# Nearest-neighbour upsampling: a first load split by partitions, and other sizes for three stores

## The chip, the cores and the metric

The kernel runs on one core of a Trainium2 chip. The time is device microseconds of that core; a shorter time is better. An execution taken by the hardware profiler has a span, from its first to its last instruction, which is a little shorter than the time.

## The reference

Every element of a float32 image batch `x[16, 64, 64, 64]` is written four times, to a 2 x 2 block of the output `[16, 64, 128, 128]`:

```
for i in range(new_h):
    for j in range(new_w):
        src_i = i // scale_factor
        src_j = j // scale_factor
        result[:, :, i, j] = x[:, :, src_i, src_j].copy()
```

There is no arithmetic. 16.78 MB are read and 67.11 MB are written.

## The kernel before

The 65,536 image rows of 64 floats are cut into 128 runs of 512 rows, one for each partition of the on-chip memory. A row is 256 B as input and becomes 1024 B of output (two output rows of 128 floats). So a load of n rows moves n x 256 B into each partition it names, and a store of k rows moves k x 1024 B out of each partition.

All of it lies in one on-chip buffer, `whole` (lines 188 to 190). Its upper part, `xt`, takes the whole input, 512 rows for each partition. The output tiles are built below it and, as input rows are used up, on top of them: even tiles at the bottom, odd tiles ending where the unread input begins (line 208). The assertion in line 209 holds two neighbouring tiles apart, and with it bounds the size of a tile and the next one together.

The loads (lines 194 to 197) are three DMAs on SyncE's queue (SP): 32 rows of all partitions, then 256, then 224. `begin_before_barrier` (line 13) puts the first three DMAs of SP (`EARLY`, line 10) ahead of the barrier with which all engines start, so that they begin at once.

The loop in line 206 runs over the nine entries of `rows` (line 181). For tile n, VectorE copies k input rows, each element twice and each row twice (`expanded`, line 199), into the tile: in one instruction (line 217), or in two where `k0` is set (lines 214 to 217). Then a DMA stores the tile (line 219). Tiles 0, 1 and the last are stored from SP's queue, the other six from ScalarE's (ACT). A DMA is issued by the sequencer of SP or ACT after it has waited for the copy. Transfers of one queue follow each other on each DMA engine, and the two queues share the 16 DMA engines.

What orders the work: a copy waits for the load that brings its rows, and for the store two tiles back, whose place it takes. In the kernel before, the 1-row copy waits for the first load, the 53-row copy for the second, and the sixth tile's for the third; the third tile's copy waits until the first store has landed. `close_early` (line 80) arranges the end of the program around the last store, and isn't touched.

Of the kernel before, what the change touches and what calls it, by code (L numbers as in the profile page):

```python
# [153 lines left out]
@with_exitstack  # L154
def kernel(
    ctx: ExitStack,
    tc: tile.TileContext,
    x: bass.AP,
    scale_factor: int,
    out: bass.AP,  # L160
):
    nc = tc.nc
    nc.at_finalize(begin_before_barrier)
    nc.at_finalize(close_early)
    P = nc.NUM_PARTITIONS
    s = int(scale_factor)
    B, C, H, W = x.shape
    R = B * C * H // P
    fdt = x.dtype

    xp = x.rearrange("b c h w -> (b c h) w").rearrange("(p r) w -> p r w", p=P)
    op = out.rearrange("b c (h hd) w -> (b c h) (hd w)", hd=s).rearrange(
        "(p r) w -> p r w", p=P
    )

    rows = [54, 38, 54, 60, 54, 62, 64, 62, 64]
    GROW = s * s
    FREE = 79
    WF = FREE * GROW * W
    assert sum(rows) == R
    mem_pool = ctx.enter_context(tc.tile_pool(name="mem", bufs=1))
    LEAD = 32
    whole = mem_pool.tile([P, LEAD + WF + R * W], fdt, name="mem")
    mem = whole[:, LEAD:]
    xt = mem[:, WF:].rearrange("p (r w) -> p r w", r=R)  # L190

    HEAD = 32
    cuts = [0, HEAD, R // 2 + HEAD, R]
    for lo, hi in zip(cuts, cuts[1:]):
        nc.sync.dma_start(out=xt[:, lo:hi], in_=xp[:, lo:hi])  # L197

    def expanded(r0, r1):
        return (  # L200
            xt[:, r0:r1].unsqueeze(2).unsqueeze(4).to_broadcast([P, r1 - r0, s, W, s])
        )

    r0 = 0
    before = (0, 0)
    for n, k in enumerate(rows):
        size = k * GROW * W
        at = 0 if n % 2 == 0 else WF + r0 * W - size
        assert at >= before[1] or at + size <= before[0]
        before = (at, at + size)  # L210
        u = mem[:, at : at + size].rearrange(
            "p (k a w b) -> p k a w b", k=k, a=s, w=W
        )
        k0 = 1 if n == 0 else 0
        if k0:
            nc.vector.tensor_copy(out=u[:, :k0], in_=expanded(r0, r0 + k0))  # L216
        nc.vector.tensor_copy(out=u[:, k0:], in_=expanded(r0 + k0, r0 + k))  # L217
        issuer = nc.sync if n in (0, 1, len(rows) - 1) else nc.scalar
        issuer.dma_start(out=op[:, r0 : r0 + k, :], in_=u)
        r0 += k  # L220
# [35 lines left out]
```

## Time and profile before

| | |
|---|---|
| median of 3 runs | 197.16 us (197.07 to 197.19) |
| span of the profiled execution | 195.8 us |
| VectorE busy | 76.9 us, 10 copies |
| DMA | 83.89 MB in 12 transfers, mean 429 GB/s |

The three runs give the time of whole executions; the profiled execution is known by its span, 1.36 us below their median. In the views, DVE is VectorE, SPq and ACTq are the sequencers of SyncE and ScalarE, POOL is GpSimd. A row with DMA names a transfer by destination and source: `mem<-in_x_dram` is a load, `out_dram<-mem` a store. The queue q1 is SP's and q10 ACT's. A share of the DMA is the mean over the 16 DMA engines. The rows with xcount group instructions of one line and shape: busy time in all, mean ns of one, then the idle time of the engine before them and what ended it. The rows of issues give KB of a transfer and the time from issue to landing.

### The profile page before, as it was taken

How to read it: one execution, taken by the hardware profiler on the slowest of the kernel's cores; microseconds unless marked ns; L12 is line 12 of the kernel's file. 1: busy time of each engine (PE TensorE's matmuls, PEld its weight loads, DVE VectorE, ACT ScalarE, POOL GpSimd, SP SyncE). 2: the span in 40 equal slices, each digit the busy share in tenths (PEclk: the TensorE clock that was granted, in tenths of full speed). 3: DMA queues.
4: the chain of work that ended last, by engine and by line, in shares of the span. 5: the costliest groups of instructions: out<-in, count | busy, mean ns of one | idle time of the engine just before them, and what ended most of it. 6: DMA issues, size and time to landing. Idle time of an engine off the chain costs nothing.

```text
span 195.8 us, 76 instructions
## 1 busy us (share of the span) xinstructions
DVE 76.9 (39%) x10; POOL 0.2 (0%) x4
## 2 busy tenths in 40 slices
DVE  0000099990029287059008805920790079000000
POOL 0000000000000000000000000000000000000000
DMA  9999989989898988999999899999999999999994
GB/s 429 429 429 429 402 375 539 398 362 542 362 435 382 551 373 362 542 402 402 402 537 407 362 542 415 415 415 415 429 429 429 429 415 558 473 435 422 429 429 214
DMA packets 1728, 83.89 MB, mean 429 GB/s; under 512 B 192, under 2 KB 192, under 8 KB 192
## 3 DMA queue, kind: packets, MB, share of 16 engines
q10 hardware_dynamic: 864, 46.66, 55.0%
q1 hardware_dynamic: 864, 37.22, 44.2%
HBM read 16.78 MB, written 67.11 MB: 429 GB/s over the span
## 4 chain that ended last, share of the span: by engine, by line
DMA 61%; DVE 24%; SPq 0%; issue 0%
DMA out_dram<-mem 49%; DVE mem L217 24%; DMA mem<-in_x_dram 12%; SPq L197 0%
## 5 line engine op out<-in xcount | busy, mean ns | idle before, releaser
L217 DVE COPY mem<-mem 128x13824 f32<-128x13824 f32 (+5 forms) x9 | 76.6, 8515 | 84.6 <-DMA out_dram<-mem 65.6
L216 DVE COPY mem<-mem 128x256 f32<-128x256 f32 x1 | 0.3, 293 | 4.8 <-DMA mem<-in_x_dram 4.8
L237 POOL MEMSET const-bfloat16-1.0<- 128x1 bf16 x1 | 0.1, 102 | 0.0
L237 POOL MEMSET const-uint8-127<- 128x1 uint8 x1 | 0.1, 101 | 0.0
L237 POOL MEMSET const-float32-0.0<- 128x1 f32 x1 | 0.1, 98 | 0.2 <-issue 0.2
L237 POOL MEMSET const-float32-1.0<- 128x1 f32 x1 | 0.1, 98 | 0.0
## 6 DMA issues: line engine op xcount, KB each, us to landing
out_dram<-mem ACTq DMA_DIRECT2D x2, 7936.0 KB, 31.6
out_dram<-mem ACTq DMA_DIRECT2D x2, 6912.0 KB, 23.7
out_dram<-mem ACTq DMA_DIRECT2D x1, 7680.0 KB, 26.1
mem<-in_x_dram SPq DMA_DIRECT2D x1, 7168.0 KB, 40.2
out_dram<-mem SPq DMA_DIRECT2D x1, 6912.0 KB, 19.0
out_dram<-mem SPq DMA_DIRECT2D x1, 4864.0 KB, 25.2
mem<-in_x_dram SPq DMA_DIRECT2D x1, 1024.0 KB, 4.8
mem<-in_x_dram SPq DMA_DIRECT2D x1, 23.7
```

What stands on the lines that cost most here:

```text
L216: nc.vector.tensor_copy(out=u[:, :k0], in_=expanded(r0, r0 + k0))
L217: nc.vector.tensor_copy(out=u[:, k0:], in_=expanded(r0 + k0, r0 + k))
L237: nc = _bacc.Bacc("TRN2", target_bir_lowering=False, num_devices=1)
```

## The change

The first 256 rows now come in two DMAs that part the partitions and not the rows: all 256 rows of partitions 0 to 15, then all 256 rows of partitions 16 to 127. The third brings the other 256 rows of all partitions. The first tile has 63 rows (54 before), the second 31 (38) and the last 62 (64). The first tile is copied in one instruction; a tile with an odd number of rows other than the first, which is the second alone, is copied as one row and the rest.

```
-    rows = [54, 38, 54, 60, 54, 62, 64, 62, 64]
+    rows = [63, 31, 54, 60, 54, 62, 64, 62, 62]
...
-    HEAD = 32
-    cuts = [0, HEAD, R // 2 + HEAD, R]
-    for lo, hi in zip(cuts, cuts[1:]):
-        nc.sync.dma_start(out=xt[:, lo:hi], in_=xp[:, lo:hi])
+    LANES = 16
+    HALF = R // 2
+    for p0, p1, lo, hi in (
+        (0, LANES, 0, HALF),
+        (LANES, P, 0, HALF),
+        (0, P, HALF, R),
+    ):
+        nc.sync.dma_start(out=xt[p0:p1, lo:hi], in_=xp[p0:p1, lo:hi])
...
-        k0 = 1 if n == 0 else 0
+        k0 = 0 if n == 0 else k % 2
         if k0:
             nc.vector.tensor_copy(out=u[:, :k0], in_=expanded(r0, r0 + k0))
         nc.vector.tensor_copy(out=u[:, k0:], in_=expanded(r0 + k0, r0 + k))
```

## The prediction

> **What bounds the kernel now.** I read the page first: engine shares, the slices of the span, the DMA queues and the chain.
>
> ```profile
> span 195.8 us, 76 instructions
> ...
> DVE 76.9 (39%) x10; POOL 0.2 (0%) x4
> ...
> DMA  9999989989898988999999899999999999999994
> GB/s 429 429 429 429 402 375 539 398 362 542 362 435 382 551 373 362 542 402 402 402 537 407 362 542 415 415 415 415 429 429 429 429 415 558 473 435 422 429 429 214
> DMA packets 1728, 83.89 MB, mean 429 GB/s; under 512 B 192, under 2 KB 192, under 8 KB 192
> ...
> q10 hardware_dynamic: 864, 46.66, 55.0%
> q1 hardware_dynamic: 864, 37.22, 44.2%
> HBM read 16.78 MB, written 67.11 MB: 429 GB/s over the span
> ```
>
> VectorE (DVE) works 39% of the span. The 16 DMA engines work 55.0 + 44.2 = 99.2% of it, in every slice but the last. Jumps in the GB/s row (375, then 539) are whole packets counted in one slice. The packet row tells how transfers are shared out: 192 small packets are 12 transfers (3 loads, 9 stores) times 16 engines, so each transfer ends on all 16; the other 1728 - 192 = 1536 are 12 x 128, one for each partition of a transfer. One engine thus carries 8 partitions of each 128-partition transfer. A view by stretches gives the steady rate (columns: stretch, length, DVE, POOL, clock, DMA share, GB/s):
>
> ```profile
> 5.00:24.00 19.00, 0.12 (x1) 0.00 (x0) 1.00 1.00 435
> 24.00:39.00 15.00, 14.86 (x2) 0.00 (x0) 1.00 0.99 428
> 166.00:190.00 24.00, 0.41 (x1) 0.00 (x0) 1.00 1.00 431
> ```
>
> Loads alone run at 435 GB/s with a share of 1.00, that is 27.2 GB/s for each engine, and stores alone at 431. All bytes at 435 GB/s need 83.89 / 0.435 = 192.9 us of the 195.8 us span: 2.9 us are left for start, slower first packets and end, and no rearrangement can win more. Losses have no such bound: any time in which the engines move less than 27.2 GB/s each is added to the end, because each later transfer gives every engine the same 8 partitions again.
>
> Next the chain in order of time, the copies by shape, and the issues:
>
> ```profile
> 0.43 23.65 DMA mem<-in_x_dram
> 24.09 0.02 issue
> 24.11 14.30 DVE mem L217
> 38.41 0.02 issue
> 38.42 19.01 DMA out_dram<-mem
> 57.44 0.02 issue
> 57.46 7.37 DVE mem L217
> 64.83 0.02 issue
> 64.85 20.38 DMA out_dram<-mem
> ```
>
> ```profile
> L217 DVE COPY mem<-mem 128x16384 f32<-128x16384 f32 x2 | 17.4, 8694 | 18.6 <-DMA out_dram<-mem 18.6
> L217 DVE COPY mem<-mem 128x15872 f32<-128x15872 f32 x2 | 16.9, 8427 | 21.0 <-DMA out_dram<-mem 21.0
> L217 DVE COPY mem<-mem 128x13824 f32<-128x13824 f32 x2 | 14.7, 7360 | 21.9 <-DMA out_dram<-mem 21.9
> L217 DVE COPY mem<-mem 128x13568 f32<-128x13568 f32 x1 | 14.3, 14286 | 19.0 <-DMA mem<-in_x_dram 19.0
> L217 DVE COPY mem<-mem 128x9728 f32<-128x9728 f32 x1 | 5.2, 5226 | 0.0
> L216 DVE COPY mem<-mem 128x256 f32<-128x256 f32 x1 | 0.3, 293 | 4.8 <-DMA mem<-in_x_dram 4.8
> ```
>
> ```profile
> mem<-in_x_dram SPq DMA_DIRECT2D x1, 7168.0 KB, 40.2
> out_dram<-mem SPq DMA_DIRECT2D x1, 4864.0 KB, 25.2
> mem<-in_x_dram SPq DMA_DIRECT2D x1, 1024.0 KB, 4.8
> mem<-in_x_dram SPq DMA_DIRECT2D x1, 23.7
> ```
>
> ```profile
> 0.00 1.33 SPq L197 DMA_DIRECT2D mem<-in_x_dram  x3
> ...
> 38.42 5.60 SPq L219 DMA_DIRECT2D out_dram<-mem  x2
> ```
>
> The chain names a 14.30 us copy, but the DMA engines are busy under it: the third load, issued near 0.9 us (three issues in 1.33 us), lands 40.2 us later, at 41.1, and the first store is issued at 38.42. That copy is covered with 41.1 - 38.4 = 2.7 us to spare. It is slow because its 53 rows are odd: 14286 / 13568 = 1.053 ns an element, where the 54-row form has 7360 / 13824 = 0.532.
>
> **The change, part by part.** *Instructions.* SP still issues three loads and three stores, ACT six stores, in the same order; VectorE still has ten copies. Transfers stay 12, issue cost is unchanged, and the packets become 16 + 112 + 128 + 9 x 128 + 192 = 1600 if the 16- and the 112-partition load still use all 16 engines. Edits to copies and stores cost nothing as long as loads run at the old rate:
>
> First copy, now 63 odd rows in one instruction: 16128 x 1.053 = 16.98 us (if it took the rate of the even form, 8.6). It waits for both first loads, 8.39 MB instead of 9.44: at the old rate they land 1.05 / 0.435 = 2.4 us before 24.09, at 21.7. So the first store goes out at 38.7 instead of 38.42, covered by the third load, whose end stays at 41.1. Without that cover each microsecond of lateness costs one.
>
> The 1-row copy (0.29 us) leaves the first tile and goes to the second: 0.29 + 7680 x 0.532 = 4.4 us instead of 5.23. Its store queues behind the first store on SP and is covered by it. The third copy waits for the first store to land and runs 7.37 us under the second store. That store lands now at 43.7 + 25.2 = 68.9 (its issue is the last 0.3 us of the two-issue row), 4.0 us after the issue at 64.85; with 31 rows for 38 it is 7 x 1024 x 128 / 0.435 = 2.1 us shorter, leaving 1.9 us for the start of a transfer. The first load, with 2.41 us of bytes, landed after 4.8, so start and landing together take 2.4 us; at worst 0.5 us shows, and I take 0. The wait for the third load moves from the sixth to the fifth tile, at 85 us, long after either landing. The last store loses 2 rows (0.6 us), but the sum of rows is the same: 0.
>
> *First load, 16 partitions.* Each engine gets one 65,536 B row, in place of eight short ones. No row of this trace shows a transfer that writes few partitions, so I bound it. If 27.2 GB/s is a limit of the engine, the load takes 65,536 / 27.2 = 2.41 us as now: 0. If it is a limit of the way into each group of 8 partitions, sixteen partitions lie in anything from 2 to 16 groups, and 16 engines share as many ways: 19.3, 9.6, 4.8 or 2.4 us. A rate in proportion to partitions, 435 / 8 = 54 GB/s, gives 19.3 too. I take four ways, the middle rung of the crowded ones (2, 4, 8): 9.6 us, +7.2, with 0 and +16.9 as ends. Every engine is in it, and the second load waits behind it on the same queue, so all of it is added.
>
> [...]
>
> *Second load, 112 partitions.* Seven rows to an engine, 7 x 2.41 = 16.9 us if nothing is shared. If the engines stay four to a way, 7 x 9.6 = 67.5. In a 128-partition load eight rows belong to each engine, and the trace shows no sharing; with seven, blocks of partitions no longer match the groups of eight, and two engines meet on one way part of the time. I take half of the time for the slowest engine: 16.9 x 1.5 = 25.3, +8.4, with 0 and +50.6 as ends. Nearest to the 435 GB/s row is 0, but the same premise that slows the first load forbids it: 16 partitions are missing, so other ways carry more than their share.
>
> [...]
>
> *Third load.* 128 partitions, eight to an engine: 19.3 us as at 435 GB/s. It covers the 17.0 us copy even then, with 2.3 us for issue and start. At the start, eight short rows become one long one: the page's first slices already show 429 GB/s, against 435 later, which over 20 us leaves 0.3 us to win; I take -0.2 (0 to -0.5).
>
> **Sum.** 195.8 + 7.2 + 8.4 - 0.2 = 211.2 us of span. The median of the runs is 197.16, 1.36 above the span; with that kept, 212.6 us.
>
> **Rivals.**
> - *No crowding* (the other side): 27.2 GB/s belongs to the engine and not to the partitions written. For it: 435 and 431 GB/s in both directions look like one engine limit. Against it: a limit on the receiving side would give the same row. Then all edits are covered, and the time is 197.2 with -0.5 to +0.5: 197.0. It decides if the first load lands within 6 us.
> - *Only the first load crowds.* If engines spread the 112 partitions well, the groups with all eight partitions left still need 8 x 2.41 = 19.3 us: +7.2 and 0 to +2.4, so 204.4 to 206.8; 205.5.
> - *Both stay four to a way.* 7.2 + 50.6: 255 us. For it: consecutive partitions on the 16 engines at any one time; against it: that needs rows dealt out one by one, which nothing in the trace shows.
> - *The slow copy comes out of cover*: if the third load's end does not move with the second load's landing, the 17.0 us copy starts late and the DMA idles. With the second load landing at 37, the copy ends at 54 and the slowest engine has load until 37 + 19.3 = 56: 2 us short of deciding. It would add 1 to 3 us to the forecast, within its range.
>
> **How the numbers follow.** Both loads crowded, as summed, with its sharing uncertain by 5 us below and 8 above (207 to 220): 0.52. Only the first: 0.20. Heavier than 220: 0.08. No crowding: 0.20, of it 0.10 faster by over 0.2%, 0.08 within 0.2% and 0.02 slower; 0.2% or 0.4 us is what a measurement of this kernel can tell from no change. So faster 0.10, same 0.08, slower 0.82. The likeliest case's own range is 207 to 220; to leave out no more than 2 in 10 the range must reach the uncrowded case too: 196.7 to 220.
>
> **What would show it.** Right: the first load lands near 12 us instead of 4.8, the second near 37 instead of 24, the first eight GB/s slices well below 429, the packet row at 1600 with 192 small ones, the first copy at 17.0 us, and later stretches unchanged at 431 to 435 GB/s but with gaps on engines that were ahead. Wrong: 435 GB/s in the first 20 us with the second load landed by 22. Fewer than 192 small packets would mean that a load doesn't use all 16 engines, and then its share would have to be told anew.

## The result, and the profile after

| | before | changed |
|---|---|---|
| median of 5 runs | 197.16 us (197.04 to 197.26) | 219.34 us (219.10 to 219.78) |
| span of the profiled execution | 195.8 us | 217.8 us (its time 219.10) |

The ratio is 1.1129, with a 95% interval of 1.1115 to 1.1142: the change costs 22.2 us. The forecast was 212.6 us, in a range of 196.7 to 220.0: the time lies inside it by 0.7 us, and 6.7 us above the forecast.

The page of the changed kernel, the rows that answer to those shown of before:

```profile
span 217.8 us, 78 instructions
...
DMA  9985999898988988999989997999898989989984
GB/s 193 193 193 193 349 205 217 337 409 385 409 379 379 557 376 385 491 396 437 501 384 440 424 488 345 488 396 536 373 409 385 554 380 396 536 373 396 536 373 210
DMA packets 1601, 83.89 MB, mean 385 GB/s; under 512 B 193, under 2 KB 193, under 8 KB 193
...
q10 hardware_dynamic: 864, 46.66, 49.5%
q1 hardware_dynamic: 736, 37.22, 49.0%
q14 instruction: 1, 0.00, 0.0%
```

The DMA engines are as busy as before, 98.5% of the span. But for eight slices, 44 us, they move 193 to 349 GB/s. A busy DMA engine isn't a fast one: a 64 KB packet of the first load took 7.9 to 9.2 us, where one of the second load took 2.42 before. The packets are 1600 as counted out, and one of another queue (q14).

The chain of waits of the changed kernel (start, length, what):

```profile
0.45 42.84 DMA mem<-in_x_dram
43.28 0.03 issue
43.31 0.02 DVEq L221
43.33 0.05 issue
43.38 16.95 DVE mem L221
60.34 0.03 DVE mem L220
60.36 21.11 DMA out_dram<-mem
81.47 0.02 issue
81.49 7.37 DVE mem L221
88.86 0.02 issue
88.89 19.06 DMA out_dram<-mem
```

and its first and third load among the issues (the last column is the time from issue to landing), with the stretch in which the second load runs (length, DVE, POOL, clock, DMA share, GB/s):

```profile
mem<-in_x_dram SPq DMA_DIRECT2D x1, 11.8
...
mem<-in_x_dram SPq DMA_DIRECT2D x1, 61.6
```

```profile
10.40:39.70 29.30, 0.00 (x0) 0.00 (x0) 1.00 0.86 215
```

(A stretch counts a packet where it starts, and the second load's first row started before 10.40 on every engine. Its 7.34 MB in about 31 us are 237 GB/s.)

The first megabyte lands after 11.8 us where it took 4.8: +7.0. The second load lands at 43.28. The third, issued near 0.9, lands at 62.5, after the first store's issue at 60.36: by the landings, the 16.95 us copy is covered still. The third load landed at 41.1 before, so 21.4 of the 22.0 us of span are lost by then.

### The profile page after: what moved, and what is told of

Read it like the earlier page. It is cut to its first block, busy times and chain, and to the rows that moved or that the text cites. A ratio compares the mean times of both kernels' runs of the same rounds, so it can differ in the third digit from the quotient of the medians.

```text
span 217.8 us, 78 instructions
## 1 busy us (share of the span) xinstructions
DVE 78.1 (36%) x10; POOL 0.2 (0%) x4
## 4 chain that ended last, share of the span: by engine, by line
DMA 64%; DVE 22%; SPq 0%; issue 0%; DVEq 0%
DMA out_dram<-mem 44%; DVE mem L221 22%; DMA mem<-in_x_dram 20%; SPq L201 0%; DVEq L221 0%; DVE mem L220 0%
## 5 line engine op out<-in xcount | busy, mean ns | idle before, releaser
L221 DVE COPY mem<-mem 128x15872 f32<-128x15872 f32 (+5 forms) x9 | 78.0, 8663 | 110.7 <-DMA out_dram<-mem 67.3
```

## The experiments

### The loads alone, and the rest alone

Two runs part the diff. One puts the loads together again and keeps all else of the change:

```
-        (0, LANES, 0, HALF),
-        (LANES, P, 0, HALF),
+        (0, P, 0, 32),
+        (0, P, 32, HALF),
         (0, P, HALF, R),
```

> The split by partitions is taken back (32 rows, 224 rows, 256 rows, each of all 128 partitions); row counts, copies and stores stay as changed. If the split alone costs the time: 197.2 us, 196.6 to 197.7, second load landing 21 to 22 us, first copy 17.0 us and covered. If the odd 63-row copy, the 31-row second store or the 62-row last store carry a part: 199 us or more.

Measured: 198.10 us beside 197.13, ratio 1.0046 (1.0029 to 1.0063), between its two cases. The other puts the three new loads into the kernel before and nothing else (its `rows` and `k0` stay):

> The kernel before with the three loads of the change and nothing else of it. If the split by partitions is the whole loss but for the 0.9 us seen with the loads merged: 218.2 to 219.2 us, second load landing at 43 us. If the changed row counts take part in the loss beyond that 0.9 us: 217 us or less.

Measured: 218.91 us, ratio 1.1103 (1.1084 to 1.1121). Its second load lands as late as in the changed kernel, or a little later (start and length, from its chain):

```profile
0.44 43.51 DMA mem<-in_x_dram
```

The split costs 21.8 us by itself; the other edits, with the loads merged, cost 0.9 to 1.0 where the forecast had nothing. In the chain with the loads merged the copy and the first store come as foretold, and the loss sits at the third store:

```profile
0.43 21.27 DMA mem<-in_x_dram
...
38.78 21.52 DMA out_dram<-mem
60.30 0.02 issue
60.32 7.37 DVE mem L221
67.69 0.02 issue
67.72 19.18 DMA out_dram<-mem
```

The copy of the fourth tile starts when the second store has landed. In the timelines of the merged kernel and of the kernel before:

```profile
69.73 8.16 DVE L221 COPY mem<-mem 128x15360 f32<-128x15360 f32 x1 [2.04 <-DMA out_dram<-mem]
```

```profile
69.03 8.16 DVE L217 COPY mem<-mem 128x15360 f32<-128x15360 f32 x1 [4.21 <-DMA out_dram<-mem]
```

From there to the third store's landing it is 67.72 + 19.18 - 69.73 = 17.2 us with the second store of 31 rows, and 64.85 + 20.38 - 69.03 = 16.2 with 38. The bytes take 16.3 at 435 GB/s. The packet records of the trace (one packet for each partition's row) show where it goes. No engine stands idle there, but with 2.0 us between the third store's issue and the landing of the second, the third store's first row takes 2.7 to 3.1 us on each of the 16 engines, 0.8 us too long on their mean. With 4.2 us, in the kernel before, every row of that store takes 2.04. Why the row is longer, no run shows.

### Where the loads lose it: partitions or memory

The first load reads 16 runs that lie 128 KB apart in memory, and writes 16 neighbouring partitions. Either could be the limit. One run keeps the partitions and changes the memory:

```
+    xn = x.rearrange("b c h w -> (b c h) w").rearrange("(p r) w -> p r w", r=R // 2)
...
+        src = xn if p1 == LANES else xp
+        nc.sync.dma_start(out=xt[p0:p1, lo:hi], in_=src[p0:p1, lo:hi])
```

> The changed kernel, but the first load fills partitions 0 to 15 from the first 4096 image rows in one piece (pieces 64 KB apart in memory instead of 128 KB), so these partitions hold other rows than the reference has there. Ways into the partitions written: nothing changes, the first load lands at 11.8 us after its issue, time 218.5 to 220 us. Memory addresses read at one time as the limit: the first load lands several us earlier or later, and the time moves by as much.

Measured: 219.44 us, first load landed after 11.6 us. Its first load among the issues:

```profile
mem<-in_x_dram SPq DMA_DIRECT2D x1, 11.6
```

Halving the distance between the pieces read makes no difference. Two runs keep the number of partitions and change which ones; that 0 to 63 would crowd and 32 to 95 not was an assumption, which no run had shown. The first half of the rows comes as partitions 0 to 63 and then the rest:

```
-        (0, LANES, 0, HALF),
-        (LANES, P, 0, HALF),
+        (0, 64, 0, HALF),
+        (64, P, 0, HALF),
```

> The first 256 rows come as partitions 0 to 63, then 64 to 127. [...] Limit of the engines alone: first load at 11 to 12 us, time 197 us. Limit in reading memory rows of one partition's run each: the same time as the load of partitions 32 to 95 in the other run, whatever it is.

or as 32 to 95 first (with `EARLY = 4`):

```
-        (0, LANES, 0, HALF),
-        (LANES, P, 0, HALF),
+        (32, 96, 0, HALF),
+        (0, 32, 0, HALF),
+        (96, P, 0, HALF),
```

> The first 256 rows come as partitions 32 to 95, then 0 to 31, then 96 to 127. Ways: 32 to 95 reach all 16 ways, one for each engine with four partitions, so the first load lands at 11 to 12 us although it has as many partitions and bytes as 0 to 63; the two loads of 32 partitions have 8 ways each and take 9.7 us each instead of 4.8, time near 207 us. Memory reads as the limit: the first load lands as late as that of partitions 0 to 63.

The first load of each among the issues, 0 to 63 and then 32 to 95:

```profile
mem<-in_x_dram SPq DMA_DIRECT2D x1, 22.8
```

```profile
mem<-in_x_dram SPq DMA_DIRECT2D x1, 13.2
```

and the rates, of the first kernel over its first half of the rows, of the second over its first load and then over the two of 32 partitions:

```profile
1.00:41.00 40.00, 0.00 (x0) 0.00 (x0) 1.00 1.01 210
```

```profile
1.40:11.70 10.30, 0.00 (x0) 0.00 (x0) 1.00 0.98 394
11.70:31.00 19.30, 0.00 (x0) 0.00 (x0) 1.00 1.00 211
```

As many partitions, bytes and engines, and half the rate or nearly the full one, by where the partitions lie. The times are 219.18 and 208.96 us, the second 2.0 us above the 207 expected. Both read runs that lie 128 KB apart in memory. So the limit is a way into the partitions that are written, and how much a load gets through depends on which partitions it names. Beside the 27.2 GB/s that each engine had in the kernel before, the sixteen engines had about what eight of them move with 0 to 63 and then 64 to 127 (210 GB/s), and nearly what all sixteen move with 32 to 95 (394, with the start counted in). Which partitions share a way, no run maps. Rows of 64 KB took 5.13 us in the load of 0 to 63, more than twice the 2.42 of such a row in the second load of the kernel before.

The first load of the changed kernel fits: its 11.8 us less the 2.4 us that start and landing took before are 9.4 us, or 112 GB/s, about what four engines move at 27.2 each (109).

### What the 112 partitions cost, and why more than the pairs

With seven rows to an engine, the author's estimate was that engines meet on a way in pairs, each in at most two of its rows. With only the pairs slowed, the load then takes 16.9 us (seven rows of 2.41) to 21.8 (two of them at half the pace) by engine. Which engines meet in which row, no run shows. The changed kernel took about 31. Four runs put one extra load in front of the merged kernel (with `EARLY = 4`) and look at it by itself:

```
+    nc.sync.dma_start(
+        out=mem[16:128, : HALF * W],
+        in_=xp[16:128, :HALF].rearrange("p r w -> p (r w)"),
+    )
```

> The merged kernel with one more load in front: 256 rows of partitions 16 to 127, seven rows for each engine, not used afterwards. At the full rate 16.9 us. With each meeting of two engines slowing these two alone, worked through row by row: 16.9 to 21.8 us by engine, so it lands near 24 us after its issue and the time is near 220 us. If a meeting holds up all sixteen: 28 to 34 us, landing at 30 to 36 us and a time of 228 to 233 us.

Measured: 229.86 us, and the load landed after 34.6:

```profile
mem<-in_x_dram SPq DMA_DIRECT2D x1, 34.6
```

So the first load, of 16 partitions, isn't what spoils the second. The next runs have 64 partitions, 34 to 97, 36 to 99 and 40 to 103 in place of 16 to 127, so that few engines meet. How many is an estimate from the rates above: 32 to 95 ran nearly free (394 GB/s), and 64 to 127, like 0 to 63, at half the rate (210), as if all sixteen met in pairs. On the way from 32 to 95 up to 64 to 127, each four partitions would make one more pair, so 34 to 97 has one pair in half of its rows:

> The merged kernel with one more load in front: 256 rows of partitions 34 to 97 into the place of the first tile, not used afterwards. By the ways, four rows for each engine, no engine meets another in the first two rows, and in the last two only two of the sixteen engines meet. If only those that meet are slowed: 14 engines at full rate, so about 400 GB/s or more from 1 to 16 us counted with the load behind it, the extra load landing near 16 us for the two. If a crowded way holds up all engines: 217 GB/s in the last third of it, and the next load starts late on all. In both cases the time is 198.1 + 9.7 + 4.8 = 212.6 us, within 1.5, as the two slow engines set the end; without any effect of two engines 207.8 us.

With 36 to 99 it is one pair in all four rows:

> The merged kernel with one more load in front: 256 rows of partitions 36 to 99, four rows for each engine, not used afterwards. [...] If only those that meet are slowed: 380 GB/s or more in the first 10 us, the pair joined after that by the engine that owns the way in the next load, so three share it, and the slowest ends at 26 us: 220 to 224 us. If one meeting holds up all sixteen: 205 to 220 GB/s in the first 20 us, 217 to 219.5 us.

With 40 to 103 it is two pairs:

> As the run with one pair, but partitions 40 to 103: two pairs meet on two ways in all four rows, 12 engines have a way alone. If only those that meet are slowed: 350 GB/s or more in the first 10 us and the same 220 to 224 us as with one pair. If two crowded ways hold up all sixteen where one does not: 205 to 240 GB/s in the first 20 us, all engines near 4.6 us a row, 217 to 219.5 us.

| extra load | engines that meet, by the estimate | time | landed after |
|---|---|---|---|
| 34 to 97 | one pair, in the last two rows | 215.34 us | 20.6 us |
| 36 to 99 | one pair, in all four rows | 222.41 us | 27.3 us |
| 40 to 103 | two pairs, in all four rows | 218.25 us | 23.0 us |

The first twenty microseconds with 36 to 99, then with 40 to 103:

```profile
1.40:21.40 20.00, 0.00 (x0) 0.00 (x0) 1.00 1.05 357
```

```profile
1.40:21.40 20.00, 0.00 (x0) 0.00 (x0) 1.00 0.98 204
```

With 36 to 99, 14 engines go through the extra load at 2.4 us a row (2.4 and, in the last two rows, 2.6 in the run of 34 to 97). The other two are the pair of the estimate: their last two rows take 6.3 to 8.0 us, and one 56 KB row of a third engine, in the next load, 6.8 instead of 2.1. That the three share a way is a reading of these lengths. Meanwhile the 56 KB rows of the others take 2.6, so they are not quite undisturbed. In the run of 34 to 97 the pair's last rows took 6.9 and 7.4 us; its expectation had two on the way to the end, and it came out 2.7 us above it. With 40 to 103 all sixteen engines are slow. The lengths of the 64 KB packets in the trace say it engine by engine (the records don't name the engine, so a packet is given to the engine whose last one ended where it begins):

```
us for a row: shortest / median / longest of the 16 engines
extra load 40 to 103    row 1  3.8 / 4.4 / 5.1    row 2  5.2 / 5.2 / 5.2
                        row 3  5.2 / 5.2 / 5.2    row 4  5.1 / 5.2 / 5.2
changed kernel, first   row 1  7.9 / 8.9 / 9.2
changed kernel, second  row 1  5.1 / 5.3 / 5.9    row 2  4.8 / 4.8 / 4.9
                        row 3  2.8 / 3.0 / 4.6    row 4  3.5 / 3.7 / 4.7
                        row 5  4.1 / 4.5 / 4.8    row 6  4.6 / 4.6 / 4.8
                        row 7  4.4 / 4.4 / 4.8
```

In the second load of the changed kernel, row 3 looks like one pair: 14 engines took 2.8 to 3.2 us and two 4.6. Row 4 lies between, at 3.5 to 4.7, perhaps because the late ones are out of step by then. In rows 1, 2 and 5 to 7 no engine is quick (4.1 us or more), as with 40 to 103 (3.8 or more). If four engines met in that run, as estimated, they held up the other twelve. By what path is open: no run separates a shared part of the way from an order in which the reads are served.

### Is there a better version in the other edits?

If the 0.9 us is the short second store, tiles of 54 and 38 rows beside the merged loads should bring it back (`k0` is 0 there, so the 54-row copy is even and quick):

```
-    rows = [63, 31, 54, 60, 54, 62, 64, 62, 62]
+    rows = [54, 38, 54, 60, 54, 62, 64, 62, 64]
```

> The merged loads again, but tiles of 54 and 38 rows first and 64 last, as before. If the 0.9 us that the merged run lost is the second store of 31 rows running out before the third can start: 197.1 to 197.4 us, and a GB/s row without the dip at the third store. If it is the boundary of the loads at 256 rows or the one-instruction copy: 198 us still.

Measured: 198.41 us, ratio 1.0067 (1.0052 to 1.0082): a miss. The long first row at the third store is gone from the trace, and another loss has come. The copy takes 7.37 us and is done early, and the first store is issued at 29.17, in the chain of this run; and its third load, of the same 8 MB, lands later than in the merged run with 63 rows (that one's row second):

```profile
29.17 29.74 DMA out_dram<-mem
```

```profile
mem<-in_x_dram SPq DMA_DIRECT2D x1, 41.6
```

```profile
mem<-in_x_dram SPq DMA_DIRECT2D x1, 40.1
```

The kernel before alone can show that, with its first copy made quick:

```
-        k0 = 1 if n == 0 else 0
+        k0 = 0
```

> The kernel before with its first tile copied in one instruction of 54 rows, which is even and takes 7.4 us instead of 14.6, so the first store is issued near 31.5 us instead of 38.4. If a first store issued long before the loads end costs the 1.3 us seen with the merged loads and 54 rows: 198.0 to 198.6 us. If the wait for the loads hides it as the chain suggests: 197.0 to 197.3 us.

Measured: 198.33 us, ratio 1.0061 (1.0046 to 1.0077). The first copy takes 7.37 us, the store goes out at 31.72, and the third load of 7 MB lands after 41.5 us, where it took 40.2:

```profile
31.72 27.05 DMA out_dram<-mem
```

```profile
mem<-in_x_dram SPq DMA_DIRECT2D x1, 7168.0 KB, 41.5
```

A quicker copy costs 1.3 us: it isn't idle time that it saves, and its store comes too early. The last try has merged loads, an odd and slow copy of 55 rows and a second store of 37:

```
-    rows = [63, 31, 54, 60, 54, 62, 64, 62, 62]
+    rows = [55, 37, 54, 60, 54, 62, 64, 62, 64]
```

> Merged loads, tiles of 55 and 37 rows first: the 55-row copy is odd, so slow, and ends near 36.6 us; the second store takes 11.2 us. If both leftovers of the merged runs are named rightly (a second store too short for the third to start behind it, 0.9 us; a first store issued long before the loads end, 1.3 us), both are gone: 196.9 to 197.5 us. If the boundary of the loads at 256 rows costs: 198 us or more.

Measured: 198.22 us, ratio 1.0056 (1.0044 to 1.0069), a miss again. The 55-row copy took 14.82 us, its first store was still early, and its third load landed after 41.4 us:

```profile
36.84 22.11 DMA out_dram<-mem
```

```profile
mem<-in_x_dram SPq DMA_DIRECT2D x1, 41.4
```

In the packets of the trace the lengthening is all in the last row of the third load, 3.6 us (median) where 2.4 is usual. Issues at 29.17, 31.72 and 36.84 us lengthen it, issues at 38.42 (before) and 38.78 (merged) do not; the last rows start at 37.9 to 38.7. That the boundary is their start is a reading of five points; no run moved it on purpose, and why the row is longer is open.

The packets also settle the boundary of the loads at 256 rows. After the first 2.5 us, the only rows clearly over their usual length in these four kernels are the third store's first (merged, 0.8 us on the mean of 16 engines) and the third load's last (the other three, 1.1 to 1.3). That is all but 0.2 us of what each kernel lost, and leaves next to nothing for the boundary. No version beat the kernel before.

## Why the prediction was right, and where it was off

- *Direction and cause* were right: the split by partitions is the loss (21.8 of 22.2 us, shown by the loads alone), by crowded ways and not by the engines' own limit or by memory (shown by 394 GB/s for 32 to 95 against 210 for the halves from 0 to 63 on, and by the nearer rows, landed after 11.6 us against 11.8). The rival without crowding would have had the second load landed by 22 us; it landed at 43. Nor did the first load crowd alone (205.5 us), or both stay four to a way (255).
- *First load*, +7.2 by four ways: 11.8 against 4.8 us, +7.0. The size was right. But four was the middle of three choices that no row of the kernel before could decide, so it was luck.
- *Second load*, +8.4: the mis-sized term. Against the merged loads, whose 256 rows were in at 0.43 + 21.27 = 21.70, both loads together cost 43.28 - 21.70 = 21.6; less 7.0 for the first, the second cost 14.6. The step that failed was that an engine is slowed only while it meets another, and this for half of the time, a share that was chosen and not counted. In five of the seven rows all sixteen ran near the 5.13 us of the load of 0 to 63 (medians of 4.4 to 5.3 us a row instead of 2.4).
- *Third load and slow copy* were right by the landings: 19.2 us between those of the second and third load, and the copy of 16.95 us within them. The packets show the last rival in part, though. On 14 of the 16 engines the third load ended at 59.9 to 60.7 us and the first store's rows began at 61.2 to 61.4, with the engine idle between. The two slowest engines, at 61.9 and 62.0, went on without a pause. At the end two engines are again 1.2 us behind the other 14 (217.4 and 216.2 us), so the pause of the 14 costs nothing that shows.
- *Copies and stores at nothing*: off by 0.9 us. The step named the third store's start behind a second store of 31 rows and allowed 0.5 us; it has 0.9 with the loads merged. In the changed kernel the third store takes as long from issue to landing (19.06 us, 19.18 merged), and its first row takes 2.9 us on the two slowest engines. Yet beside the split all the other edits add only 0.4 us (219.34 against 218.91). In the profiled run of the loads alone the same second load landed 0.7 us later (43.96 against 43.28). From there to the end of the span it is 173.7 us, and 174.5 in the changed kernel: 0.8 more.
- *Sum*: 7.0 + 14.6 + 0.9 = 22.5 against 22.2 measured and 15.4 foretold. The range held the time because 8 us were allowed above the forecast for the second load's sharing; it was all but used up.
- *A slow first copy that is merely covered*: the reading of the kernel before was incomplete. A copy that ends late enough is worth 1.3 us there, by when its store is issued.

## What to carry to other kernels

How fast a load over part of the partitions was depended on which ones it named: 112 GB/s for 0 to 15, 210 for 0 to 63 and then 64 to 127, 394 for 32 to 95, beside 435 for all. Measure such a part by itself before splitting a transfer that way, and split by rows instead where you can: the same 256 rows were in at 21.70 us in parts by rows and at 43.28 in parts by partitions. In these runs one pair of slow engines (36 to 99) left the other 14 at 2.4 us a row, but the run still had to wait for the slowest engine and took 222.41 us; with 40 to 103 all sixteen took up to 5.2 us a row, and the run 218.25. In a kernel whose DMA never rests, look at when a store is issued as well as at whether it waits: here, 2 us ahead of the landing of its predecessor was too late, and 1 us or more ahead of the last load row too early.

## What was not expected of the hardware

- A load of 40 to 103 ran at 5.2 us a row (rows 2 to 4) on all sixteen engines, where four of them meet by the estimate; loads of 36 to 99 and of 34 to 97, with two that meet, left the other 14 at 2.4 to 2.6.
- A store queued behind a load on the same queue before the load's last row has started lengthens that row by 1.2 to 1.3 us (median of the engines) in the three kernels that did it.
- The first row of a store on the other queue, issued 2.0 us before its predecessor landed, took 2.7 to 3.1 us instead of 2.04 on every engine of the merged kernel, though none stood idle; issued 4.2 us before, in the kernel before, it took 2.04.
- A load of 64 partitions reached 394 GB/s with its start counted in, when they were 32 to 95.
